# Two-layer decoder trunk: first projection started on half of x, second projection in other PSUM banks, parameter columns transposed late

## The chip, the cores and the metric

The kernel runs on one core of a Trainium2 chip. The metric is the device time of one execution in microseconds (us). The engines of the core are TensorE (PE, with its weight loads shown as PEld), VectorE (DVE), ScalarE (ACT), GpSimd (POOL) and SyncE (SP). SP does no arithmetic here; it issues DMAs. ACT and POOL issue some too. Products land in PSUM, which has eight banks of 128 partitions by 512 fp32 values; ACT and DVE carry them to SBUF ("evacuate" a bank).

## The reference

A trunk of two decoder layers for 256 positions and a model width of 1024. Each layer normalises x, multiplies it by one wide input matrix (w_in, 2615 columns), cuts the product into the inputs of three causal token mixers (a sparse one with compressed keys, one whose keys an indexer selects, a dilated one), adds their output back to x through w_out, and then runs a gated MLP with a causal convolution of width 3.

```python
def reference(x, norm1_g, w_in, cmp_pos, cmp_w1, cmp_w2, w_out, norm2_g, w_up, conv_w, conv_b, w_down, final_g):
    ...
    for i in range(DEPTH):
        h = rmsnorm(x, norm1_g[i])
        mix = hybrid_mixer(h, w_in[i], cmp_pos[i], cmp_w1[i], cmp_w2[i], cos_h, sin_h, cos_i, sin_i)
        x = x + mix @ w_out[i]
        h = rmsnorm(x, norm2_g[i])
        x = x + conv_glu_ffn(h, w_up[i], conv_w[i], conv_b[i], w_down[i])
    return rmsnorm(x, final_g)
```

In the mixers the columns of `h @ w_in` become queries, keys and values; `cmp_pos` is added to the raw keys and values of the compressed blocks, and the result goes through cmp_w1, a gelu and cmp_w2. `norm2_g` scales the MLP's input, `conv_w` and `conv_b` are the MLP's convolution.

## The kernel before

Positions lie on partitions in two row blocks t of 128. x stays in SBUF as `xr`, two tiles of 128 x 1024. For a product with w_in the columns of x have to be on partitions, so PE turns x with transposes (line 189, against `ident`), two column groups k of 128 at a time into one bank. ACT then writes the part rounded for the fast product, scaled by the norm's gain (`ahi`, line 195), and DVE the remainder (`alo`, line 196). The weights go the same way: a staging tile `st` is loaded (line 153, on SP's queue, five buffers), ACT rounds it into `hl` (line 157), DVE writes the remainder behind it (line 159). Every product is then three matmuls, high by high, high by low and low by high (`mm3`, lines 206 to 208). The factor 1/rms is left out of the product and put in at evacuation, as `rstd` or a multiple of it.

`project` computes one stretch of w_in's columns: four weight chunks of two k each, for each chunk both row blocks, so 48 matmuls into two banks, then `done(t, bank)` evacuates each. It is a generator; `dense` holds seven of them in order, and `fill(n)` runs n steps of them between other work. The first is columns 0 to 383 (`put_a0`, queries of the first mixer), the second 384 to 719 (`put_a1`), the third 1103 to 1462 (`put_i`, the indexer). All take their two banks from the pool "d", which has two. What evacuation leaves in SBUF (tiles PA, QR, PV) is rotated by position (`rope`, on DVE or POOL) and turned by PE a few steps later into a bank of the pool "t" (`turned`, line 328).

What sets the order: within an engine instructions run in the order of a list that a scheduler makes from the program and its tiles' dependencies; `tc.issue_after` (here `after`) puts an instruction behind another in it. Every engine runs its list in order and waits on semaphores. DMAs of one issuing engine stand in one queue.

The start of layer 0 is special. x comes as four loads of 256 KB: columns 0 to 511 of both row blocks first (SP and ACT), then the identity (SP) and norm1's gains (ACT), then the first weight chunk on SP, and with it the other half of x, block 0 on ACT's queue and block 1 on SP's (`other_half`). POOL issues at once the MLP's parameter rows (norm2, conv_b, conv_w), constants_f (`cf`: rope tables and masks), constants_b (`cb`), cmp_pos and later cmp_w2. PE runs 16 dummy products (`idle(16)`), turns x's first half, runs 8 more, turns the second half when it comes, and only then the first projection follows. The sums of squares (ACT and DVE) stand behind all scaled copies; `rms` and three multiples of it are on POOL. In layer 1 x is complete when the layer starts, and only the pools and the columns are the same.

`columns` turns a few parameter rows into columns: the gains of norm1 at the start, and four others (norm2 and conv_b together, cmp_pos, conv_w of either layer) at the head of `compressed`, which falls into the third projection.

Of the kernel before, what the change touches and what calls it, by code (L numbers as in the profile page):

```python
# [20 lines left out]
D = 1024  # L21
# [49 lines left out]
def trunk(ctx, tc, x, norm1_g, w_in, cmp_pos, cmp_w1, cmp_w2, w_out, norm2_g, w_up, conv_w, conv_b, w_down,  # L71
# [90 lines left out]
    def w_in_chunk(i, c0, n, then=None, behind=(None, None)):  # L162
        w = w_in[i].rearrange("(k p) c -> p k c", p=128)
        return [weight(w[:, 2 * h:2 * h + 2, c0:c0 + n], 2, n, then if h == 0 else None, behind)
                for h in range(4)]
# [39 lines left out]
    def mm3(b, ahi, alo, whi, wlo, first, last):  # L205
        PE.matmul(b, ahi, whi, start=first, stop=False)  # L206
        PE.matmul(b, ahi, wlo, start=False, stop=False)  # L207
        PE.matmul(b, alo, whi, start=False, stop=last)  # L208

    for i in range(DEPTH):  # L210

        with ExitStack() as es:
# [8 lines left out]
            first, squares = None, (None, None)  # L221
            if i == 0:
# [8 lines left out]

                def other_half():
                    nc.scalar.dma_start(xr[:, 0, 512:D], x[0, 0:128, 512:D])
                    nc.sync.dma_start(xr[:, 1, 512:D], x[0, 128:256, 512:D])

                first = w_in_chunk(0, 0, 384, other_half)
                ssq = new_ssq()
                hhi, hlo = act_pair()
                for k0 in (0, 2, 4, 6):
                    last = transposed(bank, xr, gain1[i], hhi, hlo, k0, 2, role="tsso"[k0 // 2])  # L240
                idle(8)
                for t in range(2):
                    for n in range(2):
                        junk = pj.tile([128, 512], BF, name="junkv", tag="selb")
                        xs = xr[:, t, n * 512:(n + 1) * 512]
                        if n == 0:
                            with after(last[0].ins):
                                s0 = sumsq(ssq, t, n)
                            continue
                        with after(last[1].ins):  # L250
# [758 lines left out]
```

## Time and profile before

| | |
|---|---|
| Median of 3 runs | 669.83 us (669.26 to 670.19) |
| The profiled execution | 669.9 us, of which the span shows 668.0 |
| PE busy | 645.2 us, 97% |
| DVE, ACT, POOL busy | 498.2, 374.3, 50.5 us |
| Mean granted TensorE clock | 0.992 of 2.4 GHz |

A timeline row gives the start of a piece, its length, engine and line, what it writes and reads, how many instructions it merges, and in brackets how long the engine stood idle before it and what released it. A `PEq`, `SPq` or `ACTq` is an engine's sequencer, here issuing a DMA. A row of stretches gives for each engine its busy time and count, then the granted TensorE clock (1.00 is 2.4 GHz, 0.50 is 1.2 GHz), the mean busy share of the 16 DMA engines and GB/s. Matmul ends are modelled, so the distance between starts says more than the lengths.

### The profile page before, as it was taken

To read this page: it belongs to the slowest core of one execution; us is meant where nothing else is said; L and a number is where in the kernel's file an instruction comes from. 1 tells how busy PE (TensorE), PEld (TensorE's weight loads), DVE (VectorE), ACT (ScalarE), POOL (GpSimd) and SP (SyncE) were. 2 spreads that over 40 slices of the span, in tenths; PEclk is the share of its full clock that TensorE was granted. 3 is DMA by queue.
4 is the path that set the end of the run, shared out by engine and by line. 5 is a ranking of instruction groups with operands and counts; after the bars stand their busy time and mean duration, and the time that the engine had idled before them with its cause. 6 is when DMAs were issued, how large, how long until landed. Compare 5 with 4: busy or idle time off the path is not lost. (4 is left out here: it accounts for less than half of the span.)

```text
span 668.0 us, 11736 instructions
## 1 busy us (share of the span) xinstructions
PE 645.2 (97%) x4403; PEld 580.8 (87%) x4403; DVE 498.2 (75%) x1093; ACT 374.3 (56%) x683; POOL 50.5 (8%) x120
## 2 busy tenths in 40 slices
PE   6899999999999999999998999999999999999995
PEld 5887897779999999999988888877899999999994
DVE  3888999876877666666677799987596666666653
ACT  4656686756555555554374675786665544455522
POOL 3112210000000000000110132100000000000002
PEclk7999999999999999999999999999999999999998
DMA  7595134274666666665457525134466666666601
GB/s 246 167 300 163 42 118 127 66 241 132 198 188 187 189 189 190 186 187 170 134 150 226 148 80 171 51 117 150 144 196 188 186 189 189 189 190 188 189 1 63
DMA packets 76439, 107.34 MB, mean 161 GB/s; under 512 B 3717, under 2 KB 63286, under 8 KB 76384
## 3 DMA queue, kind: packets, MB, share of 16 engines
q1 hardware_dynamic: 75280, 104.35, 51.2%
q0 software_dynamic: 496, 1.21, 0.5%
q10 hardware_dynamic: 608, 1.06, 0.5%
q8 instruction: 34, 0.56, 0.3%
q14 instruction: 21, 0.17, 0.1%
HBM read 105.55 MB, written 1.05 MB: 160 GB/s over the span
## 5 line engine op out<-in xcount | busy, mean ns | idle before, releaser
L159 DVE TENSOR_TENSOR hl<-st,hl 128x1024 fp32r<-128x1024 f32 (+3 forms) x208 | 230.9, 1120 | 101.1 <-ACT hl L157 100.5
L157 ACT CAST hl<-st 128x1024 fp32r<-128x1024 f32 (+3 forms) x208 | 197.8, 970 | 143.2 <-PE bu L898 68.1
L897 PE MATMUL bu<-alo,hl 128*128 128x256 f32 x704 | 199.8, 284 | 0.8 <-DVE alo L196 0.8
L898 PE MATMUL bu<-ahi,hl 128*128 128x256 f32 x704 | 199.0, 283 | 0.0
L896 PE MATMUL bu<-ahi,hl 128*128 128x256 f32 x704 | 198.0, 283 | 0.0
L897 PEld LDWEIGHTS bu<-alo,hl 128*128 128x128 f32 x704 | 135.1, 192 | 1.9 <-DVE alo L196 1.2
L896 PEld LDWEIGHTS bu<-ahi,hl 128*128 128x128 f32 x704 | 134.5, 192 | 1.4 <-ACT ahi L195 0.5
L898 PEld LDWEIGHTS bu<-ahi,hl 128*128 128x128 f32 x704 | 135.1, 192 | 0.0
L206 PE MATMUL bd<-hl,ahi 128*128 128x384 f32 (+3 forms) x288 | 104.5, 366 | 1.7 <-ACT gate L525 1.0
L207 PE MATMUL bd<-hl,ahi 128*128 128x384 f32 (+3 forms) x288 | 101.9, 354 | 0.0
L208 PE MATMUL bd<-hl,alo 128*128 128x384 f32 (+3 forms) x288 | 101.2, 353 | 0.0
L206 PE MATMUL bn<-hl,h_hi 128*128 128x512 f32 x176 | 68.9, 392 | 0.0
L207 PE MATMUL bn<-hl,h_hi 128*128 128x512 f32 x176 | 68.6, 391 | 0.0
L208 PE MATMUL bn<-hl,h_lo 128*128 128x512 f32 x176 | 68.4, 390 | 0.0
L206 PEld LDWEIGHTS bd<-hl,ahi 128*128 128x128 f32 x288 | 54.6, 190 | 10.7 <-issue 2.2
L207 PEld LDWEIGHTS bd<-hl,ahi 128*128 128x128 f32 x288 | 54.7, 190 | 3.0 <-issue 1.0
L208 PEld LDWEIGHTS bd<-hl,alo 128*128 128x128 f32 x288 | 54.5, 189 | 2.9 <-issue 0.7
L208 PEld LDWEIGHTS bn<-hl,h_lo 128*128 128x128 f32 x176 | 33.1, 188 | 7.3 <-DVE h_lo L920 0.4
L206 PEld LDWEIGHTS bn<-hl,h_hi 128*128 128x128 f32 x176 | 33.1, 188 | 6.7 <-ACT h_hi L919 0.5
L207 PEld LDWEIGHTS bn<-hl,h_hi 128*128 128x128 f32 x176 | 33.1, 188 | 6.0
L908 DVE SCALAR_TENSOR_TENSOR c<-a,colc,c 128x255 f32<-128x255 f32 (+1 forms) x88 | 36.7, 477 | 0.7 <-ACT c L906 0.7
L911 ACT ACTIVATE th<-c 128x512 f32<-128x512 f32 x22 | 13.9, 632 | 35.1 <-DVE c L908 35.1
(235 smaller groups left out, 736.3 us busy)
## 6 DMA issues: line engine op xcount, KB each, us to landing
st<-in_w_up_dram SPq DMA_DIRECT2D x88, 512.0 KB, 3.7
st<-in_w_down_dram SPq DMA_DIRECT2D x44, 512.0 KB, 4.3
st<-in_w_in_dram SPq DMA_DIRECT2D x40, 384.0 KB, 3.8
st<-in_w_out_dram SPq DMA_DIRECT2D x12, 512.0 KB, 3.7
st<-in_w_in_dram SPq DMA_DIRECT2D x8, 360.0 KB, 3.6
st<-in_w_in_dram SPq DMA_DIRECT2D x8, 336.0 KB, 3.4
st<-in_w_out_dram SPq DMA_DIRECT2D x8, 256.0 KB, 3.1
xr<-in_x_dram ACTq DMA_DIRECT2D x2, 256.0 KB, 5.4
```

What stands on the lines that cost most here:

```text
L157: S.copy(hv, sv)
L159: V.tensor_sub(lv, sv, hv.bitcast(F32))
L206: PE.matmul(b, ahi, whi, start=first, stop=False)
L207: PE.matmul(b, ahi, wlo, start=False, stop=False)
L208: PE.matmul(b, alo, whi, start=False, stop=last)
L896: PE.matmul(o, wa, hhi[k // 4][:, k % 4, :], start=k == 0, stop=False)
L897: PE.matmul(o, wa, hlo[k // 4][:, k % 4, :], start=False, stop=False)
L898: PE.matmul(o, wl, hhi[k // 4][:, k % 4, :], start=False, stop=k == 7)
L908: V.scalar_tensor_tensor(c[:, o + d:o + 256], a[:, o:o + 256 - d], cw[w], c[:, o + d:o + 256], op0=OP.mult, op1=OP.add)
L911: S.activation(th, c, AF.Tanh, scale=0.5)
```

## The change

1. Loads. The other half of x is issued on SP's queue alone, both blocks, right behind the first weight chunk. `cf` goes from POOL's to SP's queue, behind the fourth weight chunk. The other loads of POOL are issued only after POOL has computed rstd and its multiples: cmp_pos, cmp_w2, cb, then norm2, conv_b and conv_w.
2. First products. The scaled copies of x's first half are made first, the first weight chunk's rounding on ACT and its remainder on DVE are ordered behind the first of these copies. One step of the first projection (`fill(1)`) is placed ahead of the transposes of x's second half (`second_half`), which are ordered behind that step's last matmul. The sums of squares follow there.
3. Banks. The second projection takes its two banks from the pool "s" in both layers (`role="s"`). "s" is otherwise used by transposes at the start and by the scores later on.
4. Columns. Only cmp_pos is turned in `compressed`; norm2, conv_b and conv_w are turned when the first part of w_out's product is queued, in the dilated mixer.

The diff, cut to these:

```diff
-    for a, b, src in ((0, 16, norm2_g), (16, 60, conv_b)):
-        nc.gpsimd.dma_start(ra[a:b, :], src.rearrange("l (f p) -> (l f) p", p=128))
-    nc.gpsimd.dma_start(cf, consts_f)
-    nc.gpsimd.dma_start(cb, consts_b)
-    nc.gpsimd.dma_start(rp_, cmp_pos.rearrange("l c (j p) d -> (l c j) (p d)", p=2))
-    for i in range(DEPTH):
-        nc.gpsimd.dma_start(rc[i], conv_w[i].rearrange("w (f p) -> (w f) p", p=128))
+
+    def other_constants():
+        nc.gpsimd.dma_start(cb, consts_b)
...
-                    nc.scalar.dma_start(xr[:, 0, 512:D], x[0, 0:128, 512:D])
-                    nc.sync.dma_start(xr[:, 1, 512:D], x[0, 128:256, 512:D])
-
-                first = w_in_chunk(0, 0, 384, other_half)
+                    for t in range(2):
+                        nc.sync.dma_start(xr[:, t, 512:D], x[0, t * 128:(t + 1) * 128, 512:D])
+
                 ssq = new_ssq()
                 hhi, hlo = act_pair()
-                for k0 in (0, 2, 4, 6):
-                    last = transposed(bank, xr, gain1[i], hhi, hlo, k0, 2, role="tsso"[k0 // 2])
+                two = transposed(bank, xr, gain1[i], hhi, hlo, 0, 2, role="t")
+                first = w_in_chunk(0, 0, 384, (other_half, None, None, lambda: nc.sync.dma_start(cf, consts_f)),
+                                   [z.ins for z in two])
+                transposed(bank, xr, gain1[i], hhi, hlo, 2, 2, role="s")
                 idle(8)
...
+            def second_half(behind):
+
+                with after(behind):
+                    for k0 in (4, 6):
+                        last = transposed(bank, xr, gain1[0], hhi, hlo, k0, 2, role="so"[k0 // 2 - 2])
                 for t in range(2):
...
+            def scales():
+                nonlocal rstd
+                rstd = rms(ssq, "rstd")
+                for r, f in ((rs8, -0.125), (rs16, 0.0625), (rsh, 0.5)):
+                    last = G.tensor_scalar(r, rstd, f, None, op0=OP.mult)
+                with after(last.ins):
+                    if i == 0:
+                        nc.gpsimd.dma_start(rp_, cmp_pos.rearrange("l c (j p) d -> (l c j) (p d)", p=2))
+                    nc.gpsimd.dma_start(w2, cmp_w2[i].rearrange("c h d -> h c d"))
+                    if i == 0:
+                        other_constants()
...
-            dense += [project(0, 384, put_a0, first), project(384, 336, put_a1, behind=squares),
+            dense += [project(0, 384, put_a0, first), project(384, 336, put_a1, behind=squares, role="s"),
...
-            fill(18 + AHEAD)
+            if i == 0:
+                fill(1)
+                second_half(newest[0].ins)
+                scales()
+                fill(17 + AHEAD)
+            else:
+                scales()
+                fill(18 + AHEAD)
...
-                    columns(bank("t"), cola[:, 16:76], ra)
-                    columns(bank("t"), colp.rearrange("p l c j -> p (l c j)"), rp_)
-                    for l in range(DEPTH):
-                        columns(bank("t"), colc[:, l, :], rc[l])
+                    with after(newest[0].ins):
+                        columns(bank("t"), colp.rearrange("p l c j -> p (l c j)"), rp_)
...
             dense.append(out_part((0, 1), (2, 3), (4,)))
+            if i == 0:
+                with after(newest[0].ins):
+                    columns(bank("t"), cola[:, 16:76], ra)
+                    for l in range(DEPTH):
+                        columns(bank("t"), colc[:, l, :], rc[l])
```

What the lists of instructions look like at three places. First PE in layer 0, from the last but one dummy product on (`zero`); `xr` rows are the transposes of x's second half, 128x384 rows the first projection. Before:

```order
L227 MATMUL bd<-zero 128x256
L189 MATMUL bs<-ident,xr 128x128 x4
L189 MATMUL bo<-ident,xr 128x128 x4
L227 LDWEIGHTS zero
L227 MATMUL bd<-zero 128x256
L227 LDWEIGHTS zero
L227 MATMUL bd<-zero 128x256
L206 MATMUL bd<-hl,ahi 128x384
L207 MATMUL bd<-hl,ahi 128x384
L208 MATMUL bd<-hl,alo 128x384
```

Now:

```order
L227 MATMUL bd<-zero 128x256
L206 MATMUL bd<-hl,ahi 128x384 x2
L207 MATMUL bd<-hl,ahi 128x384
L208 MATMUL bd<-hl,alo 128x384
L206 MATMUL bd<-hl,ahi 128x384
L207 MATMUL bd<-hl,ahi 128x384
L208 MATMUL bd<-hl,alo 128x384
L189 MATMUL bs<-ident,xr 128x128 x4
L189 MATMUL bo<-ident,xr 128x128 x4
L207 MATMUL bd<-hl,ahi 128x384
```

The eight late transposes moved from ahead of the first projection to behind seven of its 48 matmuls.

Second, PE at the end of the first projection (128x384) and the head of the second (128x336). Before, the transposes of PA (an evacuated part of the first projection) stand between them, and both write "bd":

```order
L206 MATMUL bd<-hl,ahi 128x384
L207 MATMUL bd<-hl,ahi 128x384
L208 MATMUL bd<-hl,alo 128x384
L328 MATMUL bt<-ident,PA 128x128 x3
L206 MATMUL bd<-hl,ahi 128x336
L207 MATMUL bd<-hl,ahi 128x336
L208 MATMUL bd<-hl,alo 128x336
```

Now:

```order
L206 MATMUL bd<-hl,ahi 128x384
L207 MATMUL bd<-hl,ahi 128x384
L208 MATMUL bd<-hl,alo 128x384
L206 MATMUL bs<-hl,ahi 128x336
L207 MATMUL bs<-hl,ahi 128x336
L208 MATMUL bs<-hl,alo 128x336
L206 MATMUL bs<-hl,ahi 128x336
```

The second projection follows the first directly and writes "bs"; PA's transposes stand behind 18 of its matmuls.

Third, DVE from the sums of squares (`junkv`) to the first evacuation (PA): 672 and 720 columns are the weight chunks of the second and third projection. Before:

```order
L251 SCALAR_TENSOR_TENSOR junkv,ssq<-xr 128x512 x2
L159 TENSOR_TENSOR hl<-st,hl 128x672 x2
L298 TENSOR_SCALAR PA<-bd,rs_217 128x320
L298 TENSOR_SCALAR PA<-bd,rstd 128x2x64
L312 TENSOR_TENSOR rp<-QR,cf 128x80
```

Now:

```order
L258 SCALAR_TENSOR_TENSOR junkv,ssq<-xr 128x512 x2
L160 TENSOR_TENSOR hl<-st,hl 128x672 x4
L160 TENSOR_TENSOR hl<-st,hl 128x720
L311 TENSOR_SCALAR PA<-bd,rs_178 128x320
L311 TENSOR_SCALAR PA<-bd,rstd 128x2x64
```

Five remainders instead of two stand ahead of the first evacuation, the last of them for the third projection.

## Rows read from the trace of the kernel before

**Rows 1.** The page: busy time, share of the span and instructions of each engine.

```profile
PE 645.2 (97%) x4403; PEld 580.8 (87%) x4403; DVE 498.2 (75%) x1093; ACT 374.3 (56%) x683; POOL 50.5 (8%) x120
```

**Rows 2.** Timeline of PE, 0 to 45 us: start, length, what, idle before.

```profile
4.95 0.92 PE L189 MATMUL bt<-ident,xr 128*128 128x128 f32 x4
...
6.14 0.82 PE L227 MATMUL bd<-zero 128*128 128x256 bf16 x6
9.09 0.47 PE L189 MATMUL bs<-ident,xr 128*128 128x128 f32 x1 [2.12 <-DMA xr<-in_x_dram]
11.77 0.90 PE L189 MATMUL bs<-ident,xr 128*128 128x128 f32 x3 [2.21 <-DMA xr<-in_x_dram]
...
13.61 0.67 PE L206 MATMUL bd<-hl,ahi 128*128 128x384 f32 x1
...
16.79 0.34 PE L206 MATMUL bd<-hl,ahi 128*128 128x384 f32 x1
...
22.86 0.34 PE L208 MATMUL bd<-hl,alo 128*128 128x384 f32 x1
24.96 0.55 PE L328 MATMUL bt<-ident,PA 128*128 128x128 f32 x3 [1.76 <-DVE PA L298]
...
35.32 0.43 PE L206 MATMUL bd<-hl,ahi 128*128 128x360 f32 x1 [0.43 <-ACT gate L525]
```

**Rows 3.** Stretches: busy time of each engine, granted clock, DMA share, GB/s.

```profile
9.00:10.00 1.00, 0.47 (x1) 0.18 (x1) 0.00 (x0) 0.00 (x0) 0.52 (x2) 0.50 1.06 323
...
15.00:16.00 1.00, 1.00 (x5) 1.00 (x5) 0.89 (x2) 1.00 (x3) 0.00 (x0) 0.61 0.21 54
...
24.00:25.00 1.00, 0.04 (x1) 0.04 (x1) 0.65 (x2) 1.00 (x3) 0.08 (x1) 1.00 1.05 359
...
60.00:110.00 50.00, 49.63 (x333) 43.50 (x332) 48.49 (x186) 34.15 (x87) 9.53 (x24) 1.00 0.29 89
```

**Rows 4.** DMA issues of 0 to 15 us, then of the whole span: median landing.

```profile
st<-in_w_in_dram SPq DMA_DIRECT2D x4, 384.0 KB, 9.6
...
st<-in_w_in_dram SPq DMA_DIRECT2D x40, 384.0 KB, 3.8
```

**Rows 5.** Timeline of ACT, 0 to 45 us.

```profile
10.37 0.83 ACT L157 CAST hl<-st 128x768 fp32r<-128x768 f32 x1 [7.22 <-DMA st<-in_w_in_dram]
11.11 0.47 ACT L195 ACTIVATE ahi<-bt,cola 128x256 fp32r<-128x256 f32 x1
...
23.53 1.48 ACT L295 ACTIVATE QR<-bd,rs 128x640 f32<-128x640 f32 x2 [1.95 <-POOL rs L257]
```

**Rows 6.** Timeline of DVE, 0 to 45 us.

```profile
20.07 0.69 DVE L251 SCALAR_TENSOR_TENSOR junkv<-xr 128x512 bf16<-128x512 f32 x1
...
20.95 1.63 DVE L159 TENSOR_TENSOR hl<-st,hl 128x672 fp32r<-128x672 f32 x2 [0.19 <-ACT hl L157]
24.36 0.55 DVE L298 TENSOR_SCALAR PA<-bd,rs 128x320 f32<-128x320 f32 x1 [1.77 <-ACT QR L295]
24.82 0.34 DVE L298 TENSOR_SCALAR PA<-bd,rstd 128x128 f32<-128x128 f32 x1
```

**Rows 7.** Timeline of POOL, 0 to 60 us: a DMA's issue and one rope operation twice.

```profile
2.02 0.58 POOL L126 DMA_DIRECT2D rows<-in_conv_b_dram  x1
...
47.83 0.33 POOL L313 TENSOR_TENSOR rq<-PI,cf 128x72 f32<-128x72 f32 x1
...
50.37 1.13 POOL L313 TENSOR_TENSOR rq<-PI,cf 128x72 f32<-128x72 f32 x1
```

**Rows 8.** Timeline of PE, 50 to 56 us.

```profile
52.58 0.44 PE L433 MATMUL bt<-ident,kd 128*128 128x128 f32 x2 [1.57 <-ACT kd L430]
```

**Rows 9.** Timeline of PE in layer 1, 347 to 366 us.

```profile
349.40 0.55 PE L328 MATMUL bt<-ident,PA 128*128 128x128 f32 x3 [0.49 <-DVE PA L298]
...
359.35 0.63 PE L328 MATMUL bt<-ident,PA 128*128 128x128 f32 x4 [0.54 <-DVE PA L298]
360.57 0.43 PE L206 MATMUL bd<-hl,ahi 128*128 128x360 f32 x1 [0.59 <-ACT gate L525]
```

More of the change, by code (lines that the diff above doesn't have):

```diff
@@ L124, in trunk @@
     ra, rp_, rc = rows[:60, 0:128], rows[:64, 128:256], [rows[:66, 256 + 128 * i:384 + 128 * i] for i in range(DEPTH)]
[L125 to L131 removed]
+    def other_constants():
+        nc.gpsimd.dma_start(cb, consts_b)
+        for a, b, src in ((0, 16, norm2_g), (16, 60, conv_b)):
+            nc.gpsimd.dma_start(ra[a:b, :], src.rearrange("l (f p) -> (l f) p", p=128))
+        for i in range(DEPTH):
+            nc.gpsimd.dma_start(rc[i], conv_w[i].rearrange("w (f p) -> (w f) p", p=128))
     cola = keep.tile([128, 76], F32, name="cola")
@@ L160, in weight, with w_in_chunk @@
         return hv, lv
-    def w_in_chunk(i, c0, n, then=None, behind=(None, None)):
+    def w_in_chunk(i, c0, n, then=(None,) * 4, behind=(None, None)):
         w = w_in[i].rearrange("(k p) c -> p k c", p=128)
-        return [weight(w[:, 2 * h:2 * h + 2, c0:c0 + n], 2, n, then if h == 0 else None, behind)
-                for h in range(4)]
+        return [weight(w[:, 2 * h:2 * h + 2, c0:c0 + n], 2, n, then[h], behind) for h in range(4)]
     def rms(ss, name):
@@ L207, in mm3 @@
         PE.matmul(b, ahi, wlo, start=False, stop=False)
-        PE.matmul(b, alo, whi, start=False, stop=last)
+        return PE.matmul(b, alo, whi, start=False, stop=last)
     for i in range(DEPTH):
@@ L220, in trunk @@
             w2 = pj.tile([128, 2, 64], F32, name="w2")
-            first, squares = None, (None, None)
+            first, squares = None, [None, None]
             if i == 0:
@@ L241, in trunk @@
+                first = w_in_chunk(0, 0, 384, (other_half, None, None, lambda: nc.sync.dma_start(cf, consts_f)),
+                                   [z.ins for z in two])
+                transposed(bank, xr, gain1[i], hhi, hlo, 2, 2, role="s")
                 idle(8)
-                for t in range(2):
[L243 to L250, printed above, removed]
-                            s1 = V.scalar_tensor_tensor(junk, xs, 1.0, xs, op0=OP.mult, op1=OP.mult,
-                                                   accum_out=ssq[:, t, n:n + 1])
@@ L253, in trunk @@
-                squares = s0.ins, s1.ins
-            rstd = rms(ssq, "rstd")
-            rs8, rs16, rsh = (pj.tile([128, 2], F32, name=f"rs{j}") for j in range(3))
-            for r, f in ((rs8, -0.125), (rs16, 0.0625), (rsh, 0.5)):
-                G.tensor_scalar(r, rstd, f, None, op0=OP.mult)
-            nc.gpsimd.dma_start(w2, cmp_w2[i].rearrange("c h d -> h c d"))
-            def project(c0, n, done, wh=None, behind=(None, None)):
+            rstd = None
+            rs8, rs16, rsh = (pj.tile([128, 2], F32, name=f"rs{j}") for j in range(3))
@@ new lines, in second_half @@
+            def second_half(behind):
+                with after(behind):
+                    for k0 in (4, 6):
+                        last = transposed(bank, xr, gain1[0], hhi, hlo, k0, 2, role="so"[k0 // 2 - 2])
+                for t in range(2):
+                    with after(last[0].ins):
+                        squares[0] = sumsq(ssq, t, 0).ins
+                    junk = pj.tile([128, 512], BF, name="junkv", tag="selb")
+                    xs = xr[:, t, 512:D]
+                    with after(last[1].ins):
+                        squares[1] = V.scalar_tensor_tensor(junk, xs, 1.0, xs, op0=OP.mult, op1=OP.mult,
+                                                            accum_out=ssq[:, t, 1:2]).ins
@@ L261, in project @@
+            def project(c0, n, done, wh=None, behind=(None, None), role="d"):
                 wh = wh or w_in_chunk(i, c0, n, behind=behind)
-                bs = [bank("d"), bank("d")]
+                bs = [bank(role), bank(role)]
                 for half in range(4):
@@ L275, in project @@
                 yield
-            dense, later = [], []
+            dense, later, newest = [], [], [None]
             def fill(n=1000):
@@ L543, in put @@
                     P_ = tmp.tile([128, 384], F32, name="PC", tag="PX")
-                    a_put(P_, b[:, :384], r, t)
+                    a_put(P_, b[:, :384], r(), t)
                     rope(heads(P_, 6), heads(P_, 6), 8, t)
```

6 lines of the change are left out of this document (3 added, 3 removed).

## The prediction

> **What bounds the kernel now.** I read the page first: the profiled execution has a span of 668.0 us, and TensorE (PE) is busy for 645.2 us of it [rows 1]. So a change pays only where PE stands still or runs at the lower clock, and the next views are PE's timeline of the first 45 us and the stretches of the same time with the granted clock. Both show one bad place, the start. After the transposes of x's first half (columns 0 to 511) and the dummy products that end at 6.96, PE waits 2.12 us for one part of x's second half and 2.21 us for the other [rows 2]. After this pause has begun the granted clock falls: from 9 to 10 us it is 0.50, the lower level of 1.2 GHz, and it is back at 2.4 GHz only late in the microsecond from 15 to 16 (0.61), after PE had worked without a gap since 11.77 [rows 2, 3]. The first projection has its first product at 13.61 and its last one begins at 22.86. Then PE stands 1.76 us: both "d" banks are full, and their evacuation needs rstd, which comes late because the sums of squares are last. At 35.32 it waits 0.43 us again for "d", now held by the second projection [rows 2]. Further on, PE waits 1.57 us at 52.58 for the indexer's keys (kd) [rows 8], and in layer 1 the bank waits come back as 0.49, 0.54 and 0.59 us [rows 9]. From 60 to 110 us PE is busy for 49.63 of 50 us [rows 3]: what is won earlier meets no idle PE there, it shifts the whole rest.
>
> **Loads.** The four first weight loads took 9.6 us (median) to land, against 3.8 us for a load of this size over the whole kernel [rows 4]; ScalarE (ACT) sat 7.22 us until the first was there at 10.37 [rows 5]. They shared the DMA engines with a part of x on ACT's queue and with the loads that POOL issued from 1.26 on. The change takes ACT's part onto SP's queue behind the first weight chunk and all of POOL's away. Ahead of the first chunk are then only 0.58 MB, which had landed before 4.95 in this run (the first transposes need them). 0.39 MB at the 359 GB/s that this queue alone reached [rows 3] take 1.1 us, so I expect the chunk at 6 to 7.5. If sharing was not what held it, it lands at 10.3 as now; that is the other end. The Trainium skill (DMA: Bandwidth & Descriptors, Issuing engines are not separate DMA queues) says that DMAs of all issuing engines interleave on the same 16 DMA engines; 9.6 beside 3.8 us agrees, and by this rule the early end is the right one.
>
> **Part 1, the first projection starts before x is complete.** The first transposes begin at 4.95 and are through at about 5.9 (first bank) and 6.3. ACT makes three of the four scaled copies (0.47 us each [rows 5], the third waiting for DVE) until about 7.3, then the rounded weights (0.83 us) until 8.1. VectorE (DVE) makes their remainder until 9.05: two of 672 columns took 1.63 us [rows 6], so one of 768 takes 0.94. PE does two products before it and runs freely after: 46 products at 0.173 us (from 16.79 to 22.86 there are 35 steps, 6.07 us [rows 2]) are 8.0 us, the eight late transposes about 1.0. The projection ends at 18.1 instead of 23.2. Does the supply keep up? ACT has 4 casts of 0.83 and 8 copies of about 0.4, ready at 13; DVE 4 remainders of 0.94 and 8 of about 0.45, ready at 14; PE wants the last chunk at 16. **Gain 5.1 us**, of which 4.3 are the two waits and about 2 the lower clock, less 1.9 of new waiting before 9.05. If the chunk lands at 10.3, remainders end at 12.1 and 3 us of it are lost. I take off 0.4 for a landing somewhat late.
>
> **Part 2, rstd and the "s" banks.** The sums of squares end at about 15.5 on DVE, by the count above and two sums of 0.7 us. Before, the last began at 20.07, and the first evacuation of "d" followed at 23.53 [rows 5, 6], 2.8 us after its end. So the evacuation can start at about 18.2, when the products end too. PE needs it no more for the second projection, which goes into "s": the 1.76 us vanish, and so do the 0.43 at the third, since "d" is then long empty. **Gain 2.2 us.** The second projection takes what it took, 35.32 - 24.96 - 0.43 = 9.9 us with the transposes in it, and the third begins at about 28 instead of 35.3.
> What is late next: on DVE five remainders (four of 0.82 us, one of 0.91) now stand ahead of the first evacuation; from 15.5 they end at 19.6, and the columns of PA that PE turns are ready 0.9 us later (0.55 and 0.34 [rows 6]), at 20.5. PE wants them 18 products after 18.1, at 20.9. That margin is 0.4 us, and the two "t" banks turn over in the same stretch: I charge 0.5 us (0 to 1.5).
>
> **Part 3, parameters.** constants_f goes onto SP's queue behind the first four chunks (0.16 MB, 0.5 us of that queue); its readers on POOL's queue stand ahead of rms, which waits until 15.5 anyway. The other seven loads stand on POOL behind rstd's last use. An issue took 0.58 us [rows 7], so POOL is done at about 23, long before its first rope at about 37. Only the transpose of cmp_pos stays in the third projection; three transposes of 0.25 us go into the dilated part. The work is the same, so 0 (-0.3 to +0.3).
> Here a rule speaks against the change. The row of 0.58 us is from a time when DVE did nothing; beside a busy DVE one and the same POOL operation took 0.33 us once and 1.13 another time, 3.4 times as long [rows 7]. With that factor the seven issues take 14 us and end at 33, still ahead of the rope. The Trainium skill (SBUF — State Buffer, A bandwidth-pool intuition that's wrong) says that POOL-issued DMAs starve while DVE holds the port it shares with POOL, and gives about 620 ns alone and 3100 ns beside a DVE copy. By that price seven issues would take some 21 us as an estimate, until about 40; no row here shows such an issue.
>
> **Part 4, further on.** The wait for kd is set by POOL's ropes, which start when the first row block of the third projection is evacuated. In the new order both blocks of w1 products stand closer to that projection's end, and 12 instead of 14 products of the next one stand before kd. Between 0 and 1.1 us of the 1.57 go; I take 0.5. In layer 1 the same banks remove 0.49 + 0.54 + 0.59 = 1.6 us of waits [rows 9]; a wait for DVE can come back inside the second projection, so 0 to 1.6, and I take 1.2.
>
> **Sum.** 5.1 + 2.2 + 0.5 + 1.2 - 0.4 - 0.5 = 8.1 us. The profiled execution took 669.9 us (its span and 1.9 us around it), as good as the median of 669.83. **669.9 - 8.1 = 661.8 us.** All upper ends give 5.1 + 2.2 + 1.1 + 1.6 + 0.3 = 10.3, so 659.6.
>
> **Rivals.**
> *The clock falls all the same.* Between 7.2 and 9.05 PE does little. Before, it fell after 2.0 us of standing still; at 24.96, after 1.76 us, it did not [rows 2, 3]. The new pause is 0.9 us, two products and 0.55 us, so rather not. If it falls, products take 0.32 us instead of 0.173 (the pace of those from 13.61 on) until PE has worked without a gap for about the 4 us that it took before: 13 products, 2 us. Time 663.8.
> *The first chunk lands late.* The pace of the DMA engines may not be sharing but their start. Chunk at 10.3: 3 us gone, and the pause from 7.2 on is then long enough for the clock, 2 us more. The charge of 0.4 for lateness is then in it, so 8.1 + 0.4 - 5 = 3.5 us of gain remain: 666.4.
> *POOL is held.* The factor of 3.4 leaves room; from 4.5 on, seven issues of 2.6 us last until the first rope is due at 37, and at twice the row's factor kd comes late by more than PE's own work before it. I price it with what the wait for kd costs now and half as much again, 2.4 us: 664.2. Against it: only one operation in POOL's rows was that slow.
> *Nothing is won*, because DVE binds after all: it is busy for 48.49 us of the 50 from 60 to 110 [rows 3]. Against it: PE is busier, and DVE's evacuation starts 4.8 us earlier with 2.6 us of its remainders already done. If it binds, all but about 1 us stays there: 669.
> *Slower.* The evacuation of "d" stands behind the remainder of the third projection's first chunk on DVE, and that behind its load, which waits for a staging buffer until about 13. By 3.4 us as others of its size it lands at 16.5. From 18.3 on each microsecond later is one that PE waits at PA's transposes; from 26.5 on the change loses. At 28.5, 2 us slower: 672. Nothing in the rows comes near, short of SP's queue standing still.
>
> **Chances and range.** Forecast with its own spread (659.6 to 663) 0.60; clock 0.14; late chunk 0.09; POOL 0.06; nothing won 0.06; slower 0.05. The spread, clock, POOL and late chunk hold 0.89; I leave out the slow half of the late chunk's own spread, and take 659.4 to 666.5. What can be told from no change is 0.2%, 1.3 us: faster 0.90, same 0.05, slower 0.05.
>
> **What would show it.** PE's timeline: first 384-column product at about 8.1, late transposes after seven products, last product of the first projection near 18, no idle time before "bs" products, third projection from about 28. ACT's first cast near 7.3, not 10.4, shows the load. The clock row from 9 to 13 tells the second case. First evacuation of "d" on ACT near 18.2. In layer 1, no idle time before the 360-column products. The prediction is wrong if the first projection ends by 18 to 19 and the third still begins after 31, or if from 60 us on the same instruction is less than 6 us ahead of before.

## The result and the profile after

The changed kernel takes **663.22 us** (median of 4 runs, 662.68 to 663.77), the kernel before beside it 670.01 (4 runs, 669.26 to 670.60). The ratio is **0.9899, 95% interval 0.9882 to 0.9916**: 1.0% faster, 5.6 to 7.9 us. The forecast was 661.8, its range 659.4 to 666.5. The profiled execution took 662.68 us with a span of 660.9, against 669.9 and 668.0. One of the four executions of the run below that only moves 352 KB took 776.78 us at a mean granted clock of 0.752; that run's figures are those of the other three.

PE's row of the page (before: [rows 1]). PE works 3.5 us less, since fewer products ran at the lower clock; the rest of the gain is standing time.

```profile
PE 641.7 (97%) x4403; PEld 578.4 (88%) x4403; DVE 497.5 (75%) x1093; ACT 375.5 (57%) x683; POOL 50.3 (8%) x119
```

PE's timeline of the changed kernel, 0 to 48 us, to be read beside [rows 2] and [rows 8]:

```profile
8.27 0.62 PE L206 MATMUL bd<-hl,ahi 128*128 128x384 f32 x2 [1.41 <-ACT hl L158]
9.26 0.44 PE L207 MATMUL bd<-hl,ahi 128*128 128x384 f32 x1 [0.37 <-DVE hl L160]
...
18.08 0.33 PE L208 MATMUL bd<-hl,alo 128*128 128x384 f32 x1
18.25 0.31 PE L206 MATMUL bs<-hl,ahi 128*128 128x336 f32 x1
...
25.69 0.55 PE L341 MATMUL bt<-ident,PA 128*128 128x128 f32 x3 [0.88 <-DVE qrT L521]
...
28.76 0.33 PE L206 MATMUL bd<-hl,ahi 128*128 128x360 f32 x1
...
39.71 1.95 PE L607 MATMUL bo<-w,raw 128*32 128x128 f32 x64 [2.13 <-issue]
...
46.01 0.44 PE L446 MATMUL bt<-ident,kd 128*128 128x128 f32 x2 [0.99 <-ACT kd L443]
```

The last product of the first projection starts 4.78 us earlier (22.86 to 18.08), the third projection 6.56 us earlier (35.32 to 28.76), without a wait. Then there is a new idle time of **2.13 us** at the products with cmp_w1, where the kernel before had none:

```profile
43.59 1.08 PE L589 MATMUL bo<-w,raw 128*32 128x128 f32 x32
```

From here on "advance" means by how much the same PE instruction starts earlier than before, worked out from the two traces: 6.5 us at 40 us, 6.2 from 60 to 115, 5.4 from 150 to 340, 7.05 from 370 to the end.

The load behind it, in the stretches with clock and DMA share (last three columns: granted clock, DMA share, GB/s). First the kernel before, at two stretches not shown yet:

```profile
20.00:22.00 2.00, 2.00 (x14) 2.00 (x13) 1.78 (x6) 1.58 (x4) 0.90 (x3) 1.00 0.26 95
26.00:28.00 2.00, 2.00 (x17) 1.97 (x16) 2.00 (x9) 2.00 (x5) 0.00 (x0) 1.00 0.04 8
```

and the changed kernel, one stretch at the start and three later:

```profile
9.00:10.00 1.00, 0.74 (x4) 0.74 (x5) 0.60 (x2) 0.17 (x1) 0.00 (x0) 1.00 1.07 381
20.00:22.00 2.00, 2.00 (x15) 1.79 (x14) 1.86 (x7) 2.00 (x4) 1.92 (x4) 1.00 1.05 359
26.00:28.00 2.00, 2.00 (x17) 1.81 (x15) 1.94 (x3) 1.21 (x2) 0.00 (x0) 1.00 1.05 302
34.00:36.00 2.00, 2.00 (x13) 1.71 (x12) 1.09 (x5) 0.16 (x1) 0.00 (x0) 1.00 1.06 369
```

From 9 to 10 us the clock is 1.00, where [rows 3] had 0.50. But from 20 to 38 us the DMA engines are now busy without a gap (0.91 to 1.07 in every 2 us), where before they had time to spare. Here 2 MB of cmp_w1 go through SP's queue, and POOL's late loads fall into the same stretch. On ACT and DVE:

```profile
7.38 0.83 ACT L158 CAST hl<-st 128x768 fp32r<-128x768 f32 x1 [0.30 <-DMA st<-in_w_in_dram]
...
19.66 1.48 ACT L308 ACTIVATE QR<-bd,rs 128x640 f32<-128x640 f32 x2 [0.94 <-POOL rs L265]
...
23.86 0.80 ACT L158 CAST hl<-st 128x720 fp32r<-128x720 f32 x1 [0.97 <-DMA st<-in_w_in_dram]
...
35.84 0.83 ACT L158 CAST hl<-st 128x768 fp32r<-128x768 f32 x1 [2.52 <-DMA st<-in_w_in_dram]
```

```profile
36.71 0.96 DVE L160 TENSOR_TENSOR hl<-st,hl 128x768 fp32r<-128x768 f32 x1 [1.57 <-ACT hl L158]
37.70 0.23 DVE L142 COPY colp<-bt 128x64 f32<-128x64 f32 x1
...
39.04 1.09 DVE L595 TENSOR_TENSOR raw<-u,colp 128x240 f32<-128x240 f32 x2
```

The first weight chunk is there at 7.38 instead of 10.37. The chunk that lands at 35.84 (the third of the fourth projection, queued behind cmp_w1) holds ACT for 2.52 us, then DVE for 1.57, and behind DVE's remainder stand the columns of cmp_pos and `raw` (the raw keys and values with cmp_pos added), on which PE waits.

In the kernel before, the same chunk came late too, and PE did not wait. ACT and DVE there:

```profile
43.76 0.83 ACT L157 CAST hl<-st 128x768 fp32r<-128x768 f32 x1 [2.62 <-DMA st<-in_w_in_dram]
```

```profile
43.55 0.59 DVE L577 TENSOR_TENSOR raw<-u,colp 128x240 f32<-128x240 f32 x1
44.63 0.96 DVE L159 TENSOR_TENSOR hl<-st,hl 128x768 fp32r<-128x768 f32 x1 [0.49 <-ACT hl L157]
```

Both parts of `raw` (42.89 and 43.55) stood ahead of the chunk's remainder there; now two remainders (36.71 and 37.84) stand ahead of `raw`. The chunk itself comes 7.92 us earlier than before, more than PE's advance of 6.5 us. So the late chunk alone does not make this wait; it takes the turned order on DVE as well. No run tells which part of the change turned it.

In layer 1 all three bank waits of [rows 9] are gone, and the advance rises by 1.67 us there. The third projection's first product has no bracket any more:

```profile
352.88 0.32 PE L206 MATMUL bd<-hl,ahi 128*128 128x360 f32 x1
```

### The profile page after: what moved, and what is told of

Read it like the earlier page. It is cut to its first block, busy times and chain, and to the rows that moved or that the text cites. A ratio compares the mean times of both kernels' runs of the same rounds, so it can differ in the third digit from the quotient of the medians.

```text
span 660.9 us, 11729 instructions
## 1 busy us (share of the span) xinstructions
PE 641.7 (97%) x4403; PEld 578.4 (88%) x4403; DVE 497.5 (75%) x1093; ACT 375.5 (57%) x683; POOL 50.3 (8%) x119
## 3 DMA queue, kind: packets, MB, share of 16 engines
q0 software_dynamic: 448, 1.05, 0.5%
HBM read 105.55 MB, written 1.05 MB: 161 GB/s over the span
## 4 chain that ended last, share of the span: by engine, by line
PE 81%; DVE 11%; DMA 2%; issue 2%; ACT 2%; POOL 1%; POOLq 0%; DVEq 0%; ACTq 0%
PE bu L921 13%; PE bu L920 13%; PE bu L919 13%; PE bn L206 6%; PE bn L207 6%; PE bn L208 6%; PE bd L206 5%; PE bd L208 5%; PE bd L207 5%; DVE hl L160 3%; PE bs L352 2%; DMA st<-in_w_in_dram 2%; PE bt L372 2%; PE bt L341 1%; DVE acc L484 1%
## 5 line engine op out<-in xcount | busy, mean ns | idle before, releaser
L206 PE MATMUL bd<-hl,ahi 128*128 128x384 f32 (+2 forms) x256 | 92.9, 367 | 2.3 <-ACT hl L158 1.4
L207 PE MATMUL bd<-hl,ahi 128*128 128x384 f32 (+2 forms) x256 | 91.4, 357 | 0.4 <-DVE hl L160 0.4
L208 PE MATMUL bd<-hl,alo 128*128 128x384 f32 (+2 forms) x256 | 91.2, 356 | 0.0
L206 PEld LDWEIGHTS bd<-hl,ahi 128*128 128x128 f32 x256 | 48.0, 188 | 11.0 <-ACT hl L158 3.0
L207 PEld LDWEIGHTS bd<-hl,ahi 128*128 128x128 f32 x256 | 48.2, 188 | 3.6 <-issue 0.8
L208 PEld LDWEIGHTS bd<-hl,alo 128*128 128x128 f32 x256 | 48.2, 188 | 3.1 <-issue 0.9
```

The lines of the kernel that those rows point to most:

```text
L208: return PE.matmul(b, alo, whi, start=False, stop=last)
```

## The experiments

Two questions were open, with two answers each. For the first projection: **loads** (the first projection is earlier because the first chunk no longer shares the DMA engines), or **order** (because PE starts on half of x)? For the new wait: **bytes** (the full stretch from 20 to 38 us sets it) against **DVE's order** (the remainder ahead of `raw`)? The part of the banks and that of the columns were taken alone.

### Banks

Second projection in "s", alone in the kernel before:

```diff
-            def project(c0, n, done, wh=None, behind=(None, None)):
+            def project(c0, n, done, wh=None, behind=(None, None), role="d"):
...
-                bs = [bank("d"), bank("d")]
+                bs = [bank(role), bank(role)]
...
-            dense += [project(0, 384, put_a0, first), project(384, 336, put_a1, behind=squares),
+            dense += [project(0, 384, put_a0, first), project(384, 336, put_a1, behind=squares, role="s"),
```

> The kernel before with one part of the change alone: the second projection writes the two "s" banks, in both layers. If the banks carry what the prediction gave them, the three bank waits of layer 1 go (0.49 + 0.54 + 0.59 us) and the rest is 1.6 us further ahead behind them; in layer 0 PE no longer stands still between the first projection and PA's transposes, so up to 2.2 us more, 666.0 to 668.0 in all. If DVE binds behind the banks (rstd comes as late as before here, since the sums of squares are not earlier), the wait of layer 0 only moves to PA's transposes inside the second projection and layer 0 gives under 0.7 us: 667.7 to 668.5. If the banks are worth nothing anywhere: 670.

666.53 us against 669.14, ratio 0.9956 (0.9940 to 0.9972): 1.9 to 4.0 us faster. In layer 1 the advance rises by 1.75 us, all of [rows 9]. In layer 0 the waits only move, as the second case has it:

```profile
24.13 0.55 PE L328 MATMUL bt<-ident,PA 128*128 128x128 f32 x3 [0.85 <-DVE PA L298]
25.54 0.52 PE L328 MATMUL bt<-ident,QR 128*128 128x128 f32 x3 [0.40 <-ACT hl L157]
```

0.85 + 0.40 stand where 1.76 + 0.43 stood. How much of it lasts can't be read here, since x's second half landed 1.65 us earlier in this execution than in the one of [rows 2], and the granted clock was 0.55 and 0.59 from 48 to 52 us.

The changed kernel with `role="s"` taken out again:

> The changed kernel with the second projection back in the "d" banks. If the part on banks was sized rightly, the loss is about 1.7 us in layer 1 (the whole step between 340 and 370 us goes) and about 1.5 to 2.2 us in layer 0, where PE waits for the evacuation at 19.7 us: 666.5 to 667.2. If most of layer 0's bank waits had gone already because rstd comes 5 us earlier, only layer 1's 1.7 us are lost: 664.9. If the 1.67 us of layer 1 come from something other than the banks, the step there stays and the time is within 0.5 us of 663.2.

665.97 us, ratio to before 0.9952 (0.9936 to 0.9968). PE in both layers:

```profile
20.34 0.55 PE L341 MATMUL bt<-ident,PA 128*128 128x128 f32 x3 [1.88 <-DVE PA L311]
...
32.26 0.43 PE L206 MATMUL bd<-hl,ahi 128*128 128x360 f32 x1 [0.59 <-ACT gate L538]
...
344.81 0.55 PE L341 MATMUL bt<-ident,PA 128*128 128x128 f32 x3 [0.49 <-DVE PA L311]
...
355.98 0.43 PE L206 MATMUL bd<-hl,ahi 128*128 128x360 f32 x1 [0.60 <-ACT gate L538]
```

The waits of layer 0 are all back, yet of them only 0.76 us lasts beyond 150 us: the wait at cmp_w1 is 0.46 here instead of 2.13. What PE does not lose at the banks it loses there. Layer 1 gives 1.67.

### Loads and order at the start

POOL's parameter loads at the start again, everything else as changed:

```diff
+    nc.gpsimd.dma_start(rp_, cmp_pos.rearrange("l c (j p) d -> (l c j) (p d)", p=2))
+    other_constants()
...
-                    if i == 0:
-                        nc.gpsimd.dma_start(rp_, cmp_pos.rearrange("l c (j p) d -> (l c j) (p d)", p=2))
...
-                    if i == 0:
-                        other_constants()
```

> The changed kernel, but POOL issues its parameter loads (cmp_pos, constants_b, norm2, conv_b, conv_w) at the start again; constants_f stays on SP's queue and x's second half too. Theory: the loads share the 16 DMA engines, so the first weight chunk, at 7.3 us in the changed kernel, lands at 8 to 9.5 us, and the first product starts as much later; the later ones of the first projection are not short of data, so 1 to 2 us are lost, and 2 more if the granted clock falls in the longer pause: 664.2 to 667. If the part of x on ACT's queue was what held the chunk before, and not POOL's small loads, nothing changes: 663.2.

663.48 us, ratio 0.9911 (0.9882 to 0.9940): the loss of 1 to 2 us that was expected does not show, in four executions that spread from 661.83 to 665.65. The early part came as expected, the first cast at 8.04 instead of 7.38, but 384 KB are then missing from the full stretch, and the wait at cmp_w1 is 0.73. ACT and PE:

```profile
8.04 0.83 ACT L161 CAST hl<-st 128x768 fp32r<-128x768 f32 x1 [0.63 <-DMA st<-in_w_in_dram]
```

```profile
39.45 1.96 PE L606 MATMUL bo<-w,raw 128*32 128x128 f32 x64 [0.73 <-issue]
```

So POOL's late loads gain 1.24 us by the end of the first projection, and the wait at cmp_w1, 1.40 us longer, takes it back.

Block 0 of x's second half on ACT's queue, as before:

```diff
-                        nc.sync.dma_start(xr[:, t, 512:D], x[0, t * 128:(t + 1) * 128, 512:D])
+                        (nc.sync if t else nc.scalar).dma_start(xr[:, t, 512:D], x[0, t * 128:(t + 1) * 128, 512:D])
```

> The changed kernel, but block 0 of x's second half is issued on ACT's queue, as before, and only POOL's loads are late. Theory of sharing: these 256 KB then run beside the first weight chunk of 384 KB, the chunk lands 0.5 to 0.8 us later than 7.3 us and the time is 663.7 to 664.5; x's second half comes earlier, but its transposes stand behind seven products anyway. Rival: the transfer at this place is bound by its start, not by sharing, and nothing changes: 663.2. Second rival: the issue on ACT (0.6 us of ACT's time) delays the scaled copies: seen on ACT's timeline.

662.91 us, ratio 0.9901 (0.9885 to 0.9918): the same time. The sharing is there, and somewhat larger than expected:

```profile
8.29 0.83 ACT L158 CAST hl<-st 128x768 fp32r<-128x768 f32 x1 [0.99 <-DMA st<-in_w_in_dram]
```

0.91 us later than in the changed kernel; the first projection ends 0.92 us later too. Beyond 150 us 0.25 remain. Where the rest came back is open.

All of x turned ahead of the first projection:

```diff
-                fill(1)
-                second_half(newest[0].ins)
+                second_half(None)
                 scales()
-                fill(17 + AHEAD)
+                fill(18 + AHEAD)
```

> The changed kernel with the old order of the first products: all transposes of x (both halves) stand ahead of the first projection, loads and banks as in the change. It tells what of the 5 us of part 1 comes from the loads and what from starting on half of x. In the changed kernel x's second half is turned at 10.2 us, and the second weight chunk of the first projection lands at 9.8. If starting on half of x is what won, PE now stands still from 6.9 us until x's second half has landed at about 9, the clock may fall, and 1.5 to 3 us are lost (664.7 to 666.2; the latter with the lower clock). If the earlier loads alone are what won, x is there soon after the first chunk, and the loss is under 0.7 us: 663.2 to 663.9.

664.35 us, ratio 0.9926 (0.9908 to 0.9945). It is 1.1 us slower than the changed kernel by the medians, and the advance of the profiled run is 1.85 us less. The cases expected were a loss of 1.5 to 3 us and one under 0.7, and the reason given for the first does not hold:

```profile
7.69 0.33 PE L189 MATMUL bs<-ident,xr 128*128 128x128 f32 x1 [0.86 <-DMA xr<-in_x_dram]
...
8.35 0.55 PE L189 MATMUL bs<-ident,xr 128*128 128x128 f32 x3 [0.22 <-DMA xr<-in_x_dram]
...
17.29 0.33 PE L208 MATMUL bd<-hl,alo 128*128 128x384 f32 x1
...
38.78 1.79 PE L606 MATMUL bo<-w,raw 128*32 128x128 f32 x32 [2.98 <-issue]
```

```profile
40.00:42.00 2.00, 2.00 (x26) 1.19 (x22) 1.98 (x4) 1.32 (x3) 0.00 (x0) 0.50 0.39 78
```

With the new loads x's second half is there at 7.69 and 8.35, before the first weights are, so nothing is waited for; the first projection ends **0.79 us earlier** than with the changed order (17.29 against 18.08). This lead runs into the same late chunk (36.62 here), the wait at cmp_w1 is 2.98 us, and behind it the clock is at its lower level from 40 to 42 us. The loss is there, not at the start. **Order** falls: with the new loads and the old order the last product of the first projection starts 5.57 us earlier than in the kernel before. It is the loads that move it, and the clock that no longer falls.

The changed kernel without the eight dummy products:

```diff
-                idle(8)
```

> The changed kernel without the eight dummy products that stand behind the transposes of x's first half (they write nothing that is read later). PE then stands still from about 6.0 to 8.2 us instead of 6.9 to 8.2. The kernel before stood still for 2.1 us there, and its granted clock fell to 0.50 from 9 to 15.8 us. If a pause of this length is what lets the clock fall, it falls here too and about 2 us are lost (the price in the prediction's rival): 665.2. If the clock fell before only because a second pause of 2.2 us followed after four short transposes, it stays at 1.00 here, and the time is within 0.3 us of 663.2.

664.29 us, ratio 0.9921 (0.9896 to 0.9946), the advance 0.99 to 1.05 us less. The clock fell:

```profile
9.00:10.00 1.00, 1.00 (x3) 1.00 (x4) 0.29 (x1) 0.60 (x1) 0.00 (x0) 0.50 1.07 398
```

It stood at 0.50 to 0.52 from 9 to 12 us, after PE had done nothing from about 6.1 to 7.96 us, and was back at 1.00 from 12 on. So the dummies kept the clock up here. The price is half of the 2 us that the rival had.

### Columns

All four columns in the third projection, as before:

```diff
                         columns(bank("t"), colp.rearrange("p l c j -> p (l c j)"), rp_)
+                        columns(bank("t"), cola[:, 16:76], ra)
+                        for l in range(DEPTH):
+                            columns(bank("t"), colc[:, l, :], rc[l])
...
-            if i == 0:
-                with after(newest[0].ins):
-                    columns(bank("t"), cola[:, 16:76], ra)
-                    for l in range(DEPTH):
-                        columns(bank("t"), colc[:, l, :], rc[l])
```

> The changed kernel with all four parameter columns turned in the third projection again, as before the change. The trace of the changed kernel gives back 0.87 us where the three late columns stand (about 112 us), and has a new wait of 2.13 us at the products with cmp_w1 at 39.7 us. If the three early columns would be hidden in that wait, the 0.87 us come back: 662.3. If PE is busy work either way (three transposes and their copies, wherever they stand), they are only moved and the time stays within 0.2 us of 663.2. If the early copies on DVE lengthen the wait at 39.7 us, because DVE is what it waits for, the time is the same or up to 1 us worse: 663.2 to 664.2.

663.32 us, ratio 0.9914 (0.9897 to 0.9930): the same. The trace shows both sides of it:

```profile
38.35 0.27 PE L141 MATMUL bt<-ident,rows 60*128 60x60 f32 x1 [2.37 <-DVE colp L142]
...
42.18 1.95 PE L610 MATMUL bo<-w,raw 128*32 128x128 f32 x64
```

The columns are not hidden in the wait: they begin after it, and the products with cmp_w1 come 2.47 us later than in the changed kernel. A part of that is the clock: it was 0.50 from 39 to 42 us here, where the changed kernel had 1.00, and eight products of the third projection start 0.30 us apart instead of 0.165. About 1.2 us come back where the late columns would stand. The profiled run ends 1.2 us later, the medians do not differ; a gain it is not, and what the columns alone do is mixed with the clock.

### What the wait at 39.71 us is made of

The last two remainders of the fourth projection behind `raw` on DVE:

```diff
-        return [weight(w[:, 2 * h:2 * h + 2, c0:c0 + n], 2, n, then[h], behind) for h in range(4)]
+        return [weight(w[:, 2 * h:2 * h + 2, c0:c0 + n], 2, n, then[h], behind if h in range(*behind[2:], 4) else (None, None))
+                for h in range(4)]
...
+            raws = [None, None, 2]
...
-                      project(719, 384, put_b),
+                      project(719, 384, put_b, behind=raws),
...
-                    V.tensor_tensor(r[:, 0:16, 0:15],
+                    raws[1] = V.tensor_tensor(r[:, 0:16, 0:15],
```

> The changed kernel, but the last two weight remainders of the fourth projection stand behind the additions that make raw on DVE. Theory: PE's new wait of 2.13 us at 39.71 us comes from DVE, where a remainder that waits for a late weight load (landing at 35.84 on ACT, behind cmp_w1 in SP's queue) stands ahead of the columns of cmp_pos and of raw. Then raw is made about 1.5 to 2 us earlier, the wait shrinks to under 0.5 us, and of the 2 us up to 1.6 stay: 661.6 to 662.7, if the remainders are not themselves late for the fourth projection. Rival: cmp_w1 itself lands late (2 MB that are issued at 20.96 us), so the order on DVE changes nothing: the wait stays at 2 us and the time at 663.2. Second rival: the remainders are then what PE waits for a microsecond later: wait moved, 663.2.

663.21 us, ratio 0.9913 (0.9896 to 0.9930): the same time, as the second rival had it. PE:

```profile
34.97 1.08 PE L609 MATMUL bo<-w,raw 128*32 128x128 f32 x32 [0.27 <-issue]
...
41.96 0.40 PE L617 MATMUL bo<-cf,hsum 128*128 128x16 f32 x2 [1.67 <-DVE hsum L613]
...
46.34 0.44 PE L448 MATMUL bt<-ident,kd 128*128 128x128 f32 x2 [0.77 <-ACT kd L445]
```

and ACT:

```profile
36.14 0.83 ACT L158 CAST hl<-st 128x768 fp32r<-128x768 f32 x1 [4.00 <-DMA st<-in_w_in_dram]
```

The wait at cmp_w1 is nearly gone, and PE is 2.40 us ahead of the changed kernel there. But ACT now stands 4.00 us for the chunk, what is queued behind its cast (the copies that DVE needs next) comes late, and after the waits at hsum and kd PE is 0.3 us behind. The granted clock also fell in this run, to 0.50 from 43 to 46 us; since PE still waits 0.77 us for kd behind that, it can have cost little. Order alone moves the wait by two places.

352 KB out of the full stretch: POOL issues constants_b, norm2, conv_b and conv_w behind its second rope of the indexer.

```diff
-                    if i == 0:
-                        other_constants()
...
-                rope(heads(PI[:, t, 64:352], 9, 32), heads(PI[:, t, 64:352], 9, 32), 4, t)
+                turn = rope(heads(PI[:, t, 64:352], 9, 32), heads(PI[:, t, 64:352], 9, 32), 4, t)
+                if i == 0 and t == 1:
+                    with after(turn.ins):
+                        other_constants()
```

> The changed kernel, but POOL issues constants_b, norm2, conv_b and conv_w (352 KB together) behind its second rope of the indexer, at about 45.5 us, instead of at 22 us. In the changed kernel the DMA engines are busy without a gap from 20 to 38 us (share 0.91 to 1.07), and PE's new wait of 2.13 us at 39.71 us ends with what that stretch brings last. Theory: the wait is set by the bytes ahead of the weight chunk that lands at 35.8; 352 KB fewer at the 300 to 350 GB/s of that stretch are 1.0 to 1.2 us, so the chunk lands at about 34.7, the wait falls to about 1.0 us and the time to 662.0 to 662.3. Rival: DVE and ACT's order sets the wait whatever lands when: the wait stays at about 2 us, 663.2. Second rival: constants_b, first needed at 59 us, lands too late: PE waits there.

**660.90 us (660.68 to 661.59), ratio 0.9871 (0.9850 to 0.9893)**, 1.1 us less than the changed kernel in the profiled run (661.59 against 662.68). The intervals of the two ratios just overlap, so the 1.1 us rest on the traces. PE and ACT:

```profile
25.31 0.55 PE L340 MATMUL bt<-ident,PA 128*128 128x128 f32 x3 [0.45 <-DVE qrT L523]
...
38.72 1.96 PE L609 MATMUL bo<-w,raw 128*32 128x128 f32 x64 [1.50 <-issue]
```

```profile
34.84 0.83 ACT L158 CAST hl<-st 128x768 fp32r<-128x768 f32 x1 [1.90 <-DMA st<-in_w_in_dram]
```

The chunk lands 1.00 us earlier; 352 KB (of 1024 bytes) in that time would be 360 GB/s, within the 302 to 369 of the rows shown. PE gets it at two places: the wait at 25 us is 0.43 shorter, the one at cmp_w1 0.63, together 1.06, and the advance is 1.00 to 1.10 us larger to the end. So **bytes** set a part of the wait; 1.50 us of it remain, and no run took cmp_w1's 2 MB out of the stretch. constants_b landed 4.5 us after its issue at 44.47, long before its first reader at 58 us.

With x turned first as well (the edits of two of the runs above together):

> As the one before (352 KB issued at 45.5 us), and all transposes of x ahead of the first projection, in the old order. With x turned first the first projection ended 0.79 us earlier than in the changed kernel, and lost it again, with 1.87 us more, at a wait of 2.98 us at 38.8 us, behind which the granted clock fell to 0.50 from 40 to 42 us. Theory: with fewer bytes in that stretch the wait is under 2 us, the clock stays at 1.00, and the order of the first products is worth within 0.3 us either way, since both meet the same load: 662.0 to 662.6. If the 0.79 us survive, 661.2 to 661.5. If the wait is still near 3 us and the clock falls, 664.

661.63 us, ratio 0.9884 (0.9869 to 0.9900). Between 30 and 40 us PE is 1.4 us ahead of the run before it; at kd, which stood at 45.02 there, the lead is gone:

```profile
37.26 1.08 PE L608 MATMUL bo<-w,raw 128*32 128x128 f32 x32 [2.22 <-issue]
...
45.15 0.44 PE L448 MATMUL bt<-ident,kd 128*128 128x128 f32 x2 [1.73 <-ACT kd L445]
```

With `raw` first as well, and with all three:

> As the first of these (352 KB issued at 45.5 us), and the last two weight remainders of the fourth projection behind raw on DVE. In the run that had the latter alone PE's products with cmp_w1 began at 34.97 us without waiting, but ACT stood 4.00 us for the weight chunk that landed at 36.1, the casts and copies behind it came late, and PE lost the same time at hsum (0.32 + 1.67 us). Theory: what ends the stretch is the load, so the order on DVE only moves the wait, and the gain of the 352 KB (1.0 to 1.2 us) is seen here as without it: ACT's wait is about 3 us, the time 662.0 to 662.5. If order and bytes add up, the waits at hsum go altogether: 661.0 to 661.5.

> All three: 352 KB issued at 45.5 us, x turned first, raw ahead of the last two remainders on DVE. If the load at about 35 us is what the whole start runs into, this is the same as the first of these, 662.0 to 662.6. If the 0.79 us of the first projection survive because PE has other work while the load is under way, 661.0 to 661.6.

661.85 us (0.9884, 0.9866 to 0.9901) and 661.76 us (0.9886, 0.9871 to 0.9902). ACT's wait for the chunk was 1.81 us in the first of them, where about 3 were expected. The times are the same within their intervals, but the first one's holds a stretch at the lower clock:

```profile
44.52 0.44 PE L450 MATMUL bt<-ident,kd 128*128 128x128 f32 x2 [1.79 <-ACT kd L447]
```

```profile
46.00:48.00 2.00, 2.00 (x9) 2.00 (x7) 1.88 (x5) 1.35 (x3) 0.70 (x2) 0.50 0.85 309
```

PE is 0.50 us ahead of the run without this edit at kd (44.52 against 45.02) and 0.8 behind it once the clock is back. Both runs with x turned first and the 352 KB moved kept 1.00 throughout the start, and their lead at cmp_w1 is gone at kd. No order of PE's or DVE's work gave a gain in time with the 352 KB moved; what `raw` first alone would give at the full clock is open.

## Why the prediction was right, and where its steps were not

**Loads: right.** The chunk was expected at 6 to 7.5 us and its cast came at 7.38. The four loads took 6.7 us instead of the 9.6 of [rows 4]:

```profile
st<-in_w_in_dram SPq DMA_DIRECT2D x4, 384.0 KB, 6.7
```

Two runs put back one sharer each, and the chunk came 0.66 and 0.91 us later. The Trainium skill (DMA: Bandwidth & Descriptors, Issuing engines are not separate DMA queues) says that DMAs of all issuing engines interleave on the same 16 DMA engines. The trace agrees in these two numbers.

**Part 1: right in size, wrong in its cause.** 5.1 less 0.4 were predicted, 4.78 measured; the clock held. But the step called "the first projection starts before x is complete" is not what won: with the new loads, x turned first is 0.79 us better up to there. What failed is that the prediction gave the two waits for x's second half to the new order, as if it still landed for 9.09 and 11.77 us, though the same load order brought it to 7.69 and 8.35. So the size came out by luck: the loads would have given it without this step. (The split of the 5.1 into 4.3, 2 and -1.9 also makes only 4.4; the 5.1 is the difference of the two ends, 23.2 and 18.1.)

**Part 2: right, with the wrong reserve.** The third projection begins 6.56 us earlier, 1.78 more than the first; predicted were 2.2 less 0.5. The evacuation began at 19.66 instead of 18.2: the sums of squares ended 0.9 us later than forecast, and the first four of POOL's six small operations took 3.2 us behind them. PA's transposes did not wait all the same. The 0.88 us at 25.69 came from a late load (the chunk at 23.86, for which ACT stood 0.97 us), not from DVE's margin. And of this gain only 0.76 us lasts, because the wait at cmp_w1 takes the rest.

**Part 3: the step that was wrong.** "The work is the same, so 0." The columns are indeed a matter of place: before, their transposes stood at 41 to 43 us among short gaps, now at 112 to 114 us, where 0.87 us of the advance goes. But I costed the seven loads by POOL's issue time and not by the bytes they put beside SP's queue between 20 and 38 us. The run with 352 KB moved shows 1.0 to 1.1 us for them.

**Part 4: kd right, cmp_w1 missed.** kd's wait fell from 1.57 to 0.99, 0.58 us, where 0.5 was taken. I wrote that cmp_w1's products stand closer to the third projection's end and did not ask whether their operands come as much earlier: 2.13 us. Nor did I ask what stands ahead of them on DVE: the remainders of two late chunks, which stood behind them before. Up to 60 us this was mostly made up by the columns that left the stretch, by kd and by one short wait of 0.20 us, so the advance there was still 6.2. Layer 1 gave 1.67 instead of 1.2.

**Sum.** 4.8 + 1.8 at the start, -0.3 between 40 and 60 us, -0.9 at the late columns, +1.7 in layer 1: 7.1, where 8.1 was forecast. The time lies in the range, but by the prediction's own test (6 us ahead from 60 us on) it held until 115 us and not from 150 on.

**Rivals.** *Clock*: did not fall (1.00 from 9 to 10 us); without the dummies it does. *Late chunk*: no. *Nothing won* and *slower*: no; but the mechanism of "slower", a load queued behind others that holds DVE, is the one that came, 20 us later and smaller. *POOL held*: no. Its issues beside a busy DVE:

```profile
20.66 0.79 POOL L268 DMA_DIRECT2D rows<-in_cmp_pos_dram  x1
21.46 0.77 POOL L269 DMA_DIRECT2D w<-in_cmp_w_dram  x1
22.23 0.56 POOL L127 DMA_DIRECT2D cb<-in_consts_b_dram  x1
```

0.54 to 0.79 us each for the seven, with DVE busy for 1.86 of the 2 us from 20 to 22. The Trainium skill (SBUF — State Buffer, A bandwidth-pool intuition that's wrong) gives about 3100 ns for a DMA that POOL issues beside a DVE copy. No issue here took that long, beside DVE's remainders and evacuations, and the measurement decides.

## What to carry to other kernels

An advance ends at the next thing that does not move with it. When work starts earlier, draw up the bytes that the DMA queues must bring by the new times, stretch by stretch, before crediting the gain to the end: here the DMA engines went from 0.04 and 0.26 busy to full, and later edits of order only moved the wait. Look also at each in-order engine for what stands ahead of the operand: here two remainders of late chunks, where before there were none. A load that is put off is free only if the stretch into which it is put off has room; its first reader (58 us here) tells how far it may go.

## What was not expected of the hardware

PE's clock does not follow from the length of one standing time. It stayed at 1.00 after 2.13 us of standing in the changed kernel, after 2.10 us at the start with block 0 of x on ACT's queue, after 2.40 us at the products with cmp_w1 without the dummies, after 2.22 us with x turned first and the loads later, and after 2.55 us at 37.74 us in the run with all three edits. It fell to 0.50 after 2.98 us with x turned first alone, after 2.37 us with the columns early, after 1.79 us at kd with the loads later and `raw` first, after 0.32 and 1.67 us at hsum with `raw` first alone, and after some 1.9 us at the start without the dummies. Which of these a new kernel would meet can't be told from these runs. So before the times of two such runs are compared, their clock rows have to be.
